# A decoder layer on one core: rotation moved, raw weight loads moved, two retention products on split operands, three evictions on VectorE

## The chip, the cores and the metric

The kernel runs on one core of a Trainium2 chip. The metric is the device time of one execution in microseconds (us). The engines are TensorE (PE: matrix products and transposes), VectorE (DVE), ScalarE (ACT), GpSimd (POOL) and SyncE (SP). Each has its own queue and works through it in order. SP issues most of the loads; POOL issues most of the stores and some loads.

## The reference

One layer of a hybrid decoder is computed for a prompt of 1024 positions and for 8 samples of 4 positions each, with 1024 channels, all in float32:

```python
h = rms_norm(x, g_pre_mix) @ w_in      # q, k, v of attention; q, k, v, gate of retention; two merge gates
o_a = sliding-window attention (128), 8 heads on 2 key/value heads, with sinks
qr, kr = rope_ret(q_r), rope_ret(k_r)  # x * cos + rot * sin, rot swaps neighbouring channels
# retention, 4 heads, chunks of 128 positions, state s of 128 x 256 per head:
scores = (q @ k.T) * dmask
o   = scores @ v + (q @ s) * q_decay
s   = gamma**128 * s + (k * k_decay).T @ v
o_r = silu(gate) * head_rms(o)
mixed = (sigmoid(gm_a) * (o_a @ w_a_proj) + sigmoid(gm_r) * (o_r @ w_r_proj)) @ w_o
x = x + rms_norm(mixed); x = x + rms_norm(conv_ffn(rms_norm(x)))
```

The outputs are the layer's results for both groups, and the new caches and states.

## The kernel before, in words

**Split products.** Most products are made of split operands. `split` (L227) writes a rounded copy `hi` of a float32 tile with ACT, in the type fp32r, and the remainder `lo = x - hi` with DVE (the operation is in `ew`, L220, whose DVE form is line L223 of the profile). `mm3` (L254) then makes three fp32r matmuls out of them: hi times hi, hi times lo, lo times hi (L255, L256, L257). A few products, those of the retention blocks among them, are made in one float32 matmul without a split.

**The stream.** After attention, the rest of the input projection (retention's q and k, its gate, the two merge gates) is made by a generator, `stream` (L901 on). It works through 16 pairs of column blocks in the order `ORDER`. For each pair and each half `j` of the positions it makes seven products in the order A11, S1, A22, S2, A12, S4, S3 (a seven-product scheme for 2 x 2 blocks); the product A22 of a half is made inside the next half. A product is 12 matmuls of 264 columns. `adv(n)` advances the stream by n products, and the other stages call it between their own steps, so that their short products stand among the stream's. `nxt[p] = next(ws)` prepares the operand of the next pair as soon as the product that used the same buffer has been made; the eviction of the accumulators in the banks `q0`, `q1`, `q2` is ACT's (L927, L948) and DVE's (L950, L952).

**Raw weights.** `in_split` (L812) loads the two raw tiles of a pair (L819) on SP's queue, each with a `yield` after it, and then makes the seven weight operands by sums and splits (`w_split`, L331 and L223). The generator of the pair after next is called `coming`. Up to the end of the sample group's blocks the raw tiles take turns in two buffers, from then on in three. The first raw tile is last read by the sum `a21 = a11 - a21`, which is part of the S3 step; the second by the split of `a22`.

**Rotation.** A half of a retention q/k pair is finished in `post_qk` (L853): SP loads the neighbouring channels into two `sh` tiles (L860) when `flush()` is called, at the S2 product of the next half. The second step, `turned`, is put on the list `LATER`: six DVE operations (times cosine, times sine, sum, for q and for k) and a store to `qk_d` on POOL's queue (L868). It is called at the S1 product of the half after.

**The sample group's retention** (`sample`, L1040) runs among products of the stream, first head after `adv(4)` and `adv(20)`. It loads states from DRAM, splits them into `s0s`, and adds products with them (L1078, L1083).

**The prompt's retention** has 32 blocks (4 heads of 8 chunks). `front` makes the scores and transposes k in one bank (L1164, L1165), DVE multiplies by the mask into `sT` (L1167), ACT by the decay into `kt` (L1169). `middle` makes three float32 products of 256 columns: scores with v (L1177), q with the state (L1179), k with v (L1181); DVE updates the state (L1184, L1186), and `finish` normalizes with ACT and POOL (L1017 to L1022). `tail` transposes back (L1028) and multiplies by the gate (L1200). In the loop, block g+1 has its `front` before block g has its `middle`, with four products of the stream per block. `load_qk` (L1138) and `load_v` (L1145) are issued three blocks ahead, into five buffers each.

**The attention projection** (`attn_proj`, L779) makes eight half tiles `y_a` in three chunks each; ACT evicts each chunk (L786) out of two PSUM buffers.

**Order.** A planner goes over the whole program, takes what is ready by its own model of the durations, earlier program text first, and so fixes the order on every engine's queue; it also places the waits. What is written next to each other need not stay so.

Of the kernel before, what the change touches and what calls it, by code (L numbers as in the profile page):

```python
# [10 lines left out]
F32R = mybir.dt.float32r  # L11
# [7 lines left out]
P = 128  # L19
# [101 lines left out]
def trunk(ctx, tc, I, O):  # L121
# [657 lines left out]
    def attn_proj(mm):  # L779
        def src(r0):  # L780
            return w_a[r0:r0 + 256, 256 * mm:256 * mm + 256].rearrange("(g d) n -> d g n", d=64)
        w = weights(4, 256, [(lambda r: r[0:64], src(0)), (lambda r: r[64:128], src(256))])
        for half in range(2):
            y = p2.tile([P, T], F32, name="y_a", bufs=2)
            for c0, n in CHUNKS[1:] + CHUNKS[:1]:
                S.copy(out=y[:, c0:c0 + n], in_=gemm_chunk(w, actA, c0, n, 4, half * P, ps_a()))  # L786
            st.dma_start(out=gm_d[2 * mm + half], in_=y)
# [113 lines left out]
    def stream():  # L901
# [8 lines left out]
        for i, n in enumerate(ORDER):  # L910
            for j in range(2):
# [17 lines left out]
                for p in (A11, S1, A22, S2, A12, S4, S3):  # L929
                    if p == A22:  # L930
                        if last is not None:
                            product(A22, *last)
                        if j == 0 and i:
                            ops[A22] = next(ws)
                            ws = coming
                            if i + 1 < len(ORDER):
                                next(ws)
# [15 lines left out]
                    if p == S2:  # L953
                        flush()
                    if p == S1 and LATER:
                        LATER.pop()()
# [6 lines left out]
                    if j and i + 1 < len(ORDER):  # L963
                        nxt[p] = next(ws)
                        if p == S4 and i + 2 < len(ORDER):
# [131 lines left out]
    adv(20)  # L1097
# [35 lines left out]
    def load_qk(g):  # L1133
# [3 lines left out]
        qks[g] = ST("qk", (P, 2, P), bufs=5)  # L1137
        ld.dma_start(out=qks[g], in_=qk_d[h].rearrange("i p t -> p i t")[:, :, cols(tt)])  # L1138

    def load_v(g):  # L1140
# [3 lines left out]
        vts[g] = ST("vt", (P, 256), bufs=5)  # L1144
# [14 lines left out]
    def front(g, dm):  # L1159
# [6 lines left out]
        sT = ST("sT", (P, P), bufs=2)  # L1166
        V.tensor_tensor(out=sT, in0=ps[:, :P], in1=dm, op=mult)  # L1167
        kt = ST("kt", (P, P), bufs=2)
        S.mul(kt, ps[:, P:2 * P], kdec[:, 0, h:h + 1])  # L1169
        return ps, sT, kt, vt, q  # L1170

    def middle(g, ps, sT, kt, vt, q):
# [4 lines left out]
        TE.matmul(po, sT, vt, start=True, stop=tt == 0)  # L1177
# [3 lines left out]
        TE.matmul(pk, kt, vt, start=True, stop=True)  # L1181
# [53 lines left out]
    def ahead(g):  # L1235
# [4 lines left out]
        load_qk(g + 3)  # L1240
        load_v(g + 3)
        return front(g, state["dm"])

    for g in range(3):
        load_qk(g)
    for g in range(3):
        load_v(g)
    adv(0)
    coming, behind = ahead(0), None
    for g in range(NBLK):  # L1250
        f, coming = coming, ahead(g + 1)
# [3 lines left out]
        m = middle(g, *f)  # L1255
        adv(1)
# [6 lines left out]
    adv(len(ORDER) * 14 - 8 - 82 - 4 * NBLK - 1)  # L1263
# [526 lines left out]
```

## Time and profile before

| | us |
|---|---|
| median of 3 runs | 1656.74 (1656.53 to 1758.46) |
| profiled execution | 1658.69 |
| its span, first to last instruction | 1656.9 |
| PE busy | 1626.7 (98%) |
| DVE busy | 1205.9 (73%) |
| ACT busy | 863.6 (52%) |
| POOL busy | 446.3 (27%) |

The page and the answers of the trace come from the one profiled execution; a line such as L223 is a line of the kernel. "Busy" of PE overlaps, since matmuls are pipelined: the distance of their starts tells what one costs. Waits name the engine and line that waited, behind the arrow what released it. The stages that the change touches lie at these places of the span: the attention projection from about 237 us, the stream and the sample group's retention from about 300 to 450 us, the prompt's retention from about 450 to 686 us.

### The profile page before, as it was taken

The page shows a single profiled execution, that of the slowest core. Times are in us where ns is not written, and L with a number is a line of the kernel's source. Part 1 is how long each engine was busy: PE and PEld are TensorE (multiplying, and loading weights), DVE is VectorE, ACT ScalarE, POOL GpSimd, SP SyncE. Part 2 cuts the span into 40 slices and gives each one's busy share as a digit, 9 for nine tenths or more (in the row PEclk, how much of TensorE's full clock was granted, in tenths as well). Part 3 has the DMA queues.
Part 4 walks back from the last instruction along what each step waited for, and adds up shares of the span by engine and source line. Part 5 has one row for each costly group of instructions (what it writes and reads, how often), then busy time and mean ns, then how long its engine had stood idle before and what let it go on. Part 6 is the DMA issues. An engine that isn't in the chain of part 4 may idle for free.

```text
span 1656.9 us, 32509 instructions
## 1 busy us (share of the span) xinstructions
PE 1626.7 (98%) x12551; PEld 1589.6 (96%) x12551; DVE 1205.9 (73%) x2035; ACT 863.6 (52%) x1882; POOL 446.3 (27%) x654
## 2 busy tenths in 40 slices
PE   8999999999999999999999999999999999999997
PEld 7999999999999999999789999999999999999997
DVE  7878749688565655569748988988988988445476
ACT  6565634456565655564424655555555556443343
POOL 4232431012233332243312422321231322111111
PEclk9999999999999999999999999999999999999999
DMA  7212235556677665697422245454545548766664
GB/s 201 65 49 71 72 80 193 185 187 191 207 230 235 197 216 156 209 309 234 157 89 89 59 148 173 161 162 160 182 136 177 173 150 253 237 196 198 194 186 145
DMA packets 275852, 278.22 MB, mean 168 GB/s; under 512 B 23552, under 2 KB 234784, under 8 KB 275681
## 3 DMA queue, kind: packets, MB, share of 16 engines
q1 hardware_dynamic: 241937, 159.58, 33.2%
q0 software_dynamic: 33760, 116.57, 20.1%
q8 instruction: 98, 1.61, 0.4%
q14 instruction: 57, 0.47, 0.1%
HBM read 184.24 MB, written 87.49 MB: 164 GB/s over the span
## 4 chain that ended last, share of the span: by engine, by line
PE 71%; DMA 3%; DVE 1%; issue 1%; ACT 0%; POOL 0%; DVEq 0%; POOLq 0%; SPq 0%
PE ps_m L255 10%; PE ps_m L257 10%; PE ps_m L256 10%; PE ps_t L256 8%; PE ps_t L255 8%; PE ps_t L257 8%; PE ps_q L255 4%; PE ps_q L257 4%; PE ps_q L256 4%; PE ps_b L1177 1%; PE ps_a L1181 1%; PE ps_b L1179 1%; DMA w_raw<-in_w_in 1%; DMA t<-in_w_o 1%; DMA vt<-v_d 0%
## 5 line engine op out<-in xcount | busy, mean ns | idle before, releaser
L255 PE MATMUL ps_t<-xh,w_hi 128*128 128x264 f32 (+2 forms) x524 | 148.9, 284 | 0.0
L223 DVE SCALAR_TENSOR_TENSOR w_lo<-w_raw,w_hi 128x1024 fp32r<-128x1024 f32 x82 | 103.6, 1268 | 62.0 <-ACT w_hi L228 57.2
L256 PE MATMUL ps_t<-xl,w_hi 128*128 128x264 f32 (+2 forms) x524 | 148.7, 284 | 0.0
L257 PE MATMUL ps_t<-xh,w_lo 128*128 128x264 f32 (+2 forms) x524 | 148.0, 283 | 0.0
L257 PE MATMUL ps_m<-xh,w_lo 128*128 128x264 f32 x512 | 145.4, 284 | 0.6 <-DVE w_lo L223 0.6
L255 PE MATMUL ps_m<-xh,w_hi 128*128 128x264 f32 x512 | 145.8, 285 | 0.0
L256 PE MATMUL ps_m<-xl,w_hi 128*128 128x264 f32 x512 | 145.4, 284 | 0.0
L223 DVE SCALAR_TENSOR_TENSOR w<-w_raw,w 128x512 fp32r<-128x512 f32 x152 | 104.2, 685 | 38.4 <-ACT w L331 38.0
L1537 DVE SCALAR_TENSOR_TENSOR c_out<-u_ext,fconst,c_out 128x1024 f32<-128x1024 f32 x96 | 121.9, 1280 | 2.1 <-ACT c_out L1533 0.3
L255 PE MATMUL ps_q<-xh,w 128*128 128x264 f32 x384 | 114.2, 297 | 3.1 <-DVE pair L950 3.1
L255 PE MATMUL ps_q<-ex,w 128*128 128x264 f32 x384 | 114.0, 297 | 0.6 <-DVE pair L952 0.6
L228 ACT CAST w_hi<-w_raw 128x1024 fp32r<-128x1024 f32 x62 | 65.2, 1052 | 92.7 <-PE ps_t L256 80.0
L256 PE MATMUL ps_q<-ex,w 128*128 128x264 f32 x384 | 110.6, 288 | 0.0
L256 PE MATMUL ps_q<-xl,w 128*128 128x264 f32 x384 | 110.5, 288 | 0.0
L257 PE MATMUL ps_q<-xh,w 128*128 128x264 f32 x384 | 110.4, 288 | 0.0
L257 PE MATMUL ps_q<-ex,w 128*128 128x264 f32 x384 | 109.8, 287 | 0.0
L331 ACT CAST w<-w_raw 128x512 fp32r<-128x512 f32 x152 | 94.7, 623 | 15.7 <-PE ps_q L257 8.2
L257 PEld LDWEIGHTS ps_t<-xh,w_lo 128*128 128x128 f32 x524 | 98.7, 188 | 0.0
L256 PEld LDWEIGHTS ps_t<-xl,w_hi 128*128 128x128 f32 x524 | 98.6, 188 | 0.0
L255 PEld LDWEIGHTS ps_t<-xh,w_hi 128*128 128x128 f32 x524 | 98.6, 188 | 0.0
L257 PEld LDWEIGHTS ps_m<-xh,w_lo 128*128 128x128 f32 x512 | 96.3, 188 | 0.8 <-DVE w_lo L223 0.8
L255 PEld LDWEIGHTS ps_m<-xh,w_hi 128*128 128x128 f32 x512 | 96.2, 188 | 0.0
(450 smaller groups left out, 6072.6 us busy)
## 6 DMA issues: line engine op xcount, KB each, us to landing
w_raw<-in_w_up SPq DMA_DIRECT2D x48, 512.0 KB, 4.3
w_raw<-in_w_in SPq DMA_DIRECT2D x42, 512.0 KB, 4.2
w_raw<-s_d SPq DMA_DIRECT2D x60, 256.0 KB, 4.1
t_d<-t POOLq DMA_DIRECT2D x24, 528.0 KB, 4.0
t<-t_d POOLq DMA_DIRECT2D x24, 528.0 KB, 4.9
t<-in_w_down SPq DMA_DIRECT2D x48, 256.0 KB, 5.2
s_d<-t POOLq DMA_DIRECT2D x24, 512.0 KB, 3.6
w_raw<-in_w_down SPq DMA_DIRECT2D x36, 256.0 KB, 5.1
```

The lines of the kernel that those rows point to most:

```text
L223: pinned(V.scalar_tensor_tensor(out=out, in0=in0, scalar=1.0, in1=in1, op0=mult, op1=op))
L228: pinned(S.copy(out=hi, in_=src))
L255: TE.matmul(ps, wh, xh, start=start, stop=False, **kw)
L256: TE.matmul(ps, wh, xl, start=False, stop=False, **kw)
L257: TE.matmul(ps, wl, xh, start=False, stop=stop, **kw)
L331: S.copy(out=t[:, 0:4], in_=src)
L1177: TE.matmul(po, sT, vt, start=True, stop=tt == 0)
L1179: TE.matmul(po, q, state["s"], start=False, stop=True)
L1181: TE.matmul(pk, kt, vt, start=True, stop=True)
L1537: V.scalar_tensor_tensor(out=c[:, NS:], in0=u[:, g, NU + t:NU + t + SEQ], scalar=sc[t], in1=c[:, NS:], op0=mult, op1=add)
```

## The change

- `attn_proj`: the three chunks of the first half tile are evicted by DVE; the other 21 by ACT as before.
- `stream`: the second step of the rotation is called at the S2 product, ahead of `flush()`, and no longer at S1.
- `stream`: the second raw tile of the pair after next is loaded right after the S3 operand is prepared (the first one is loaded one product earlier, at S4, as before), and no longer at the next half's A22.
- The sample group starts after 22 products instead of 20; what is left after the prompt's blocks is two products fewer.
- Retention blocks: `sT` and `kt` become the two halves of one tile `sk`. A new function `parts` splits `v` and `sk`; it is called for the next block after the `middle` of the present one. Its four results have one buffer each. The products L1177 and L1181 become `mm3`, three fp32r matmuls each; the product with the state stays in float32.
- `load_qk` and `load_v` run two blocks ahead instead of three, with four and three buffers instead of five each.

```diff
@@ attn_proj
-                S.copy(out=y[:, c0:c0 + n], in_=gemm_chunk(w, actA, c0, n, 4, half * P, ps_a()))
+                ps = gemm_chunk(w, actA, c0, n, 4, half * P, ps_a())
+                if mm or half:
+                    S.copy(out=y[:, c0:c0 + n], in_=ps)
+                else:
+                    V.tensor_copy(out=y[:, c0:c0 + n], in_=ps)
@@ stream
                             ops[A22] = next(ws)
                             ws = coming
-                            if i + 1 < len(ORDER):
-                                next(ws)
...
                     if p == S2:
+                        if LATER:
+                            LATER.pop()()
                         flush()
-                    if p == S1 and LATER:
-                        LATER.pop()()
...
                         nxt[p] = next(ws)
+                        if p == S3 and i + 2 < len(ORDER):
+                            next(coming)
                         if p == S4 and i + 2 < len(ORDER):
                             coming = in_split(ORDER[i + 2])
                             next(coming)
@@
-    adv(20)
+    adv(22)
@@ load_qk, load_v
-        qks[g] = ST("qk", (P, 2, P), bufs=5)
+        qks[g] = ST("qk", (P, 2, P), bufs=4)
...
-        vts[g] = ST("vt", (P, 256), bufs=5)
+        vts[g] = ST("vt", (P, 256), bufs=3)
@@ front
-        sT = ST("sT", (P, P), bufs=2)
-        V.tensor_tensor(out=sT, in0=ps[:, :P], in1=dm, op=mult)
-        kt = ST("kt", (P, P), bufs=2)
-        S.mul(kt, ps[:, P:2 * P], kdec[:, 0, h:h + 1])
-        return ps, sT, kt, vt, q
-
-    def middle(g, ps, sT, kt, vt, q):
+        sk = ST("sk", (P, 2 * P), bufs=2)
+        V.tensor_tensor(out=sk[:, :P], in0=ps[:, :P], in1=dm, op=mult)
+        S.mul(sk[:, P:], ps[:, P:2 * P], kdec[:, 0, h:h + 1])
+        return ps, sk, vt, q
+
+    def parts(ps, sk, vt, q):
+        s, v = ([ST(n + b, (P, 256), F32R) for b in "hl"] for n in ("s", "v"))
+        split(*v, vt)
+        split(*s, sk)
+        return ps, s, v, q
+
+    def middle(g, ps, sk, vt, q):
...
-        TE.matmul(po, sT, vt, start=True, stop=tt == 0)
+        mm3(po, *(x[:, :P] for x in sk), *vt, True, tt == 0)
...
-        TE.matmul(pk, kt, vt, start=True, stop=True)
+        mm3(pk, *(x[:, P:] for x in sk), *vt, True, True)
@@ the loop over blocks
-        load_qk(g + 3)
-        load_v(g + 3)
+        load_qk(g + 2)
+        load_v(g + 2)
...
-    for g in range(3):
+    for g in range(2):
         load_qk(g)
-    for g in range(3):
+    for g in range(2):
         load_v(g)
     adv(0)
-    coming, behind = ahead(0), None
+    f, behind = parts(*ahead(0)), None
     for g in range(NBLK):
-        f, coming = coming, ahead(g + 1)
+        coming = ahead(g + 1)
...
         m = middle(g, *f)
+        f = parts(*coming) if coming else None
...
-    adv(len(ORDER) * 14 - 8 - 82 - 4 * NBLK - 1)
+    adv(len(ORDER) * 14 - 8 - 84 - 4 * NBLK - 1)
```

## The prediction

> **What bounds the kernel now.** I read the page first, then the waits of TensorE's own queue, then the stretches of time by stage, then the order of events around each of those waits.
>
> ```profile
> PE 1626.7 (98%) x12551; PEld 1589.6 (96%) x12551; DVE 1205.9 (73%) x2035; ACT 863.6 (52%) x1882; POOL 446.3 (27%) x654
> PE 71%; DMA 3%; DVE 1%; issue 1%; ACT 0%; POOL 0%; DVEq 0%; POOLq 0%; SPq 0%
> ```
>
> TensorE (PE) is busy 98% of the span, and the chain that ended last is PE nearly throughout. So the change can pay in two ways only: less PE work, or fewer of the few PE waits.
>
> ```profile
> PE ps_q L255 <- DVE pair L950: 3.1, 2, 2.1
> PE ps_b L1078 <- DVE s0s L223: 2.1, 1, 2.1
> PE ps_b L1028 <- ACT o L1022: 1.5, 1, 1.5
> PE ps_a L255 <- ACT y_a L786: 1.5, 1, 1.5
> PE ps_q L255 <- DVE pair L952: 0.6, 1, 0.6
> ```
>
> Columns: who waited for whom, us in total, times, longest. These five are the longest waits of PE in the stages that the change touches, 8.8 us together. The stages themselves:
>
> ```profile
> 330.00:360.00 30.00, 26.93 (x209) 26.48 (x208) 25.32 (x47) 14.84 (x39) 4.51 (x7) 0.94 0.55 185
> 395.00:430.00 35.00, 31.99 (x250) 31.70 (x251) 21.68 (x40) 23.06 (x59) 6.00 (x9) 0.96 0.64 200
> 475.00:570.00 95.00, 95.00 (x728) 92.86 (x728) 53.13 (x118) 57.10 (x142) 39.09 (x67) 1.00 0.66 207
> 570.00:685.00 115.00, 115.00 (x886) 112.69 (x885) 65.75 (x140) 63.85 (x159) 35.88 (x60) 1.00 0.54 173
> ```
>
> Columns: length, then PE, PEld, DVE, ACT and POOL busy, the granted clock, DMA share. The last two rows are the prompt's retention blocks: PE never idle, VectorE (DVE) at 56 and 57%, ScalarE (ACT) at 60 and 56%. The first two, inside the sample group's stage, have PE idle for 3 us each, and a clock below 1: 30 us x 0.06 = 1.8 us and 35 us x 0.04 = 1.4 us are lost to it. The one wait of 2.1 us in each stretch stands ahead of it:
>
> ```profile
> 351.02 0.56 PE L1078 MATMUL ps_b<-s0s,q 128*64 128x256 f32 x3 [2.09 <-DVE s0s L223]
> 351.59 0.28 PE L256 MATMUL ps_q<-xl,w 128*128 128x264 f32 x1
> 351.71 0.31 PE L257 MATMUL ps_q<-xh,w 128*128 128x264 f32 x1
> 352.04 0.42 PE L256 MATMUL ps_q<-xl,w 128*128 128x264 f32 x1
> 352.26 0.42 PE L257 MATMUL ps_q<-xh,w 128*128 128x264 f32 x1
> ```
>
> Matmuls that start 0.12 us apart are 0.22 us apart soon after the wait. I price such a wait at 2.1 + 1.6 = 3.7 us (1.6 is the mean of 1.8 and 1.4). The Trainium skill, "TensorE: Matmul & The Clock Gate", Part 1 on the clock gate, says the clock halves after an idle window of about 3.4 us; by it a 2.1 us wait would cost 2.1 us alone. The granted clock of these stretches speaks against that.
>
> **Split operands in two block products.** Each of 32 blocks has three fp32 products, of which the first (L1177) and third (L1181) become three fp32r matmuls each; the second, with the state, stays.
>
> ```profile
> 527.00 0.59 PE L1177 MATMUL ps_b<-vt,sT 128*128 128x256 f32 x2
> 527.43 0.59 PE L1179 MATMUL ps_b<-state,qk 128*128 128x256 f32 x2
> 527.86 0.59 PE L1181 MATMUL ps_a<-vt,kt 128*128 128x256 f32 x2
> 534.68 0.59 PE L1177 MATMUL ps_b<-vt,sT 128*128 128x256 f32 x2
> 431.89 0.28 PE L1083 MATMUL ps_a<-v,kb 128*128 128x256 f32 x1
> 432.01 0.28 PE L256 MATMUL ps_q<-ex,w 128*128 128x264 f32 x1
> ```
>
> Durations overlap in the pipeline; starts count. One fp32 product takes 0.43 us (527.00 to 527.43). An fp32r matmul of the same 256 columns, L1083, gives way after 0.12 us. Three are 0.36 us, so 0.07 us is saved per product, 0.14 us per block, 4.5 us in 32 blocks. With 0.118 to 0.125 us as what rounding leaves of 0.12, the bounds are 3.5 and 4.9 us. As PE is the bound there, this goes straight into the span.
>
> The price is two ACT casts and two DVE subtractions of 128x256 per block (the merged operand `sk` replaces two writes by two). Nearest rows:
>
> ```profile
> 682.09 0.47 ACT L1022 ACTIVATE o<-ps_b,rs 128x256 f32<-128x256 f32 x1 [0.24 <-POOL rs L1021]
> 685.84 0.42 ACT L228 CAST xh<-z 128x264 fp32r<-128x264 f32 x1
> 686.94 0.43 DVE L223 SCALAR_TENSOR_TENSOR xl<-z,xh 128x264 fp32r<-128x264 f32 x1
> 679.47 0.59 PE L1177 MATMUL ps_b<-vt,sT 128*128 128x256 f32 x2
> ```
>
> That is 64 x 0.43 = 27.5 us of DVE and 64 x 0.42 = 27 us of ACT in some 245 us (32 blocks of 7.68 us, 527.00 to 534.68), which takes both to about 68 to 70%. Nothing waits in the loop: the splits stand behind the block's normalization, which ends 3.1 us after the block's first product (682.56 against 679.47); two casts and the last subtraction make it 4.4 us; the next block's products come at 7.6 us. The single buffers of the split halves are free by then too, because the state update ahead of them on DVE already waits for the same third product. Cover 3.2 us; if it is gone, PE waits for what is missing, once a block.
>
> Shorter leads: a `vt` is now wanted about 2.5 blocks (19 us) and a `qk` 2 blocks (15 us) after its issue; issue to landing took
>
> ```profile
> DMA to landing us min/median/max: 2.3/3.8/8.3
> DMA to landing us min/median/max: 2.2/4.0/11.5
> ```
>
> (`vt`, then `qk`). Both fit; zero.
>
> **Entry of the retention.** The first `vt` has no such lead. It used to be read by PE alone, in the block's first product. Now ACT's in-order queue reads it right behind `front`, with all of ACT's evictions behind it and, on DVE, bank evictions L950 and L952. A DVE that stood waiting for a landing shows both ends:
>
> ```profile
> 449.94 0.69 DVE L223 SCALAR_TENSOR_TENSOR s<-w_raw 128x512 f32<-128x512 f32 x1 [3.12 <-DMA w_raw<-in_w_in]
> 425.54 0.69 DVE L223 SCALAR_TENSOR_TENSOR s<-w_raw 128x512 f32<-128x512 f32 x1 [5.25 <-DMA w_raw<-in_w_in]
> ```
>
> The 3.12 us cost PE nothing, the 5.25 us became the 2.1 us wait for L950 and its clock, 3.7 us. The longest `vt` landing was 8.3 us. I take +1.0 us, nearer the lower row, since ACT may have other work ahead of it; bounds 0 and +3.7. I exclude a gain: nothing is removed there but two early loads.
>
> **Rotation's second step later.**
>
> ```profile
> 349.03 0.71 DVE L223 SCALAR_TENSOR_TENSOR pair<-pair,rcos 128x528 f32<-128x528 f32 x1 [4.56 <-DMA sh<-pair]
> 350.28 0.68 DVE L223 SCALAR_TENSOR_TENSOR s0s<-s,s0s 128x512 fp32r<-128x512 f32 x1
> 345.86 0.62 ACT L228 CAST s0s<-s 128x512 fp32r<-128x512 f32 x1
> 343.79 1.18 SPq L860 DMA_DIRECT2D sh<-pair  x2
> ```
>
> DVE stood 4.56 us waiting for the neighbour rows, with the sample's state split queued behind it, whose other half ACT had ready at 346.5; that split is what PE waited for at 351.02. The step now comes two products (2 x 1.46 us: 12 starts of 0.12) later. But it also frees the two `sh` buffers later, so the loads of the next half, which SP issues as they come free, move with it: of 2.9 us hardly one is left as lead. The sample blocks move by the same two products (22 for 20), so the order of this step against them need not change either. Best case: this wait with its clock and one of the L950 waits (3.1 - 2.1 = 1.0 us) go, -4.7 us. Worst: nothing. I take -2.0, a little under half. Its store on GpSimd's queue moves alike with the normalizations' steps there, so zero. Two products fewer stand between the last block and the end of the stream; PE's one wait there is the 0.6 us for L952, so zero, at most the two products, 2.9 us.
>
> **Raw weights earlier.** In the retention the second load comes three products earlier; DVE's waits for it there cost no PE time (clock and PE are full). In the stage before, only two raw buffers exist, and the load at 418 us, the cause of the 5.25 us wait, was issued as its buffer came free:
>
> ```profile
> 418.30 0.37 SPq L819 DMA_DIRECT2D w_raw<-in_w_in  x1
> 417.58 0.69 DVE L223 SCALAR_TENSOR_TENSOR w<-w_raw,w 128x512 fp32r<-128x512 f32 x1 [1.58 <-ACT w L331]
> ```
>
> (417.58 + 0.69 = 418.27.) It can't come sooner. Zero, at best -3.7 us by chance of order.
>
> **First projection tile on VectorE.** PE waited 1.5 us for ACT's eviction at
>
> ```profile
> 250.24 0.86 ACT L786 COPY y_a<-ps_a 128x384 f32<-128x384 f32 x2
> 249.89 0.55 DVE L223 SCALAR_TENSOR_TENSOR qS<-o,qS 128x32 fp32r<-128x32 f32 x4 [6.71 <-ACT qS L228]
> ```
>
> DVE is idle 6.71 us before, so it can evict earlier; but the product that waits also needs the sample columns split at 249.89 to 250.44. I take -0.3 us; bounds -1.5 and +0.5 (evictions queued behind the split). The three evictions, about 0.43 us each as on ACT, delay the operand sums behind them on DVE by 1.3 us; the projection's other 21 chunks hide that.
>
> **Sum:** -4.5 + 1.0 - 2.0 - 0.3 = -5.8 us. The profiled execution took 1658.69 us, its span 1656.9 us and 1.8 us around it; it lies 1.95 us over the median of 1656.74. So 1652.9 us there, and 1651 us as a median.
>
> **Rivals.**
>
> First, the stalls go as a whole: -4.9 - 4.7 - 1.5 - 3.7 = -14.8, 1642 us. For it: each hangs on the order of a few instructions. Against it: the raw load's buffer and the sh buffers above.
>
> Second, the moved steps change nothing, because the planner already interleaves the six operations of the rotation with others (the split follows two of them at 350.28), and the entry costs its whole 3.7 us: -4.5 + 3.7, 1656 us. The later steps then don't do what they say.
>
> Third, slower: in the sample's stage the second raw load now stands ahead of the split that frees its buffer, by three products, 4.4 us, on SP's in-order queue. State loads and `qk` loads queue behind; if they land late, a split of `s0s` is late as at 350.28, 3.7 us each time. The sample's 56 products span four steps of 14, so up to four times: +14.8 - 5.8 = +9, 1666 us; from two times on it decides. Against it:
>
> ```profile
> SPq L819 <- DVE w7x L223: 57.3, 6, 19.4
> SPq L1038 <- DMA out_ret_sample<-s: 28.6, 9, 9.1
> ```
>
> SP waits up to 19.4 us on raw buffers already, without a PE wait that names a state load.
>
> **Numbers.** Chances: forecast (1646 to 1655) 0.50, first rival 0.15, second 0.22, slower 0.13. The range 1642 to 1660 us takes in the bounds: below, the first rival; above, -3.5 with the entry's +3.7 and 2.9 us at the end of the stream, +3.1. Over 2% is 33 us, about what a measurement of this kernel can tell from no change; no case reaches it, and I leave 0.02 faster and 0.03 slower for order upset elsewhere.
>
> **What will show it.** L1177 and L1181 with three starts of 0.12 us each, a block of 7.54 us; DVE near 69% there with no PE wait for L223 on the split halves. PE waits at the entry for L950 or L927 behind a `vt` landing: my +1.0. The wait for `s0s` and the lower clock near 350 us: gone or still there decides the rotation. A block pitch of 7.7 us or more, or SP holding state loads, would prove me wrong.

## The result, and the profile after

The changed kernel takes 1666.04 us (median), the kernel before 1656.74 us in the runs made beside it: a ratio of 1.0055, 95% interval 1.0041 to 1.0068. It is slower by 9 us, where a gain of 6 us was forecast; that is within 2%, as forecast, but 6 us above the upper end of the range. Executions that stand far above the others of their kernel, as the 1758.46 us in the table of before, are left out of all ratios. The profiled execution of the changed kernel took 1666.49 us, its span is 1664.7 us. In the changed kernel's lines L950 and L952 (bank evictions by DVE) have become L952 and L954, L927 is L931, L786 is L788 with DVE's form at L790, and the merge's L1287 to L1304 are L1297 to L1314.

The page of the changed kernel, busy time and the chain of waits:

```profile
PE 1626.6 (98%) x12615; PEld 1590.9 (96%) x12615; DVE 1229.7 (74%) x2102; ACT 875.4 (53%) x1943; POOL 454.1 (27%) x654
PE 85%; DVE 6%; DMA 5%; issue 2%; ACT 2%; SPq 1%; POOL 0%; DVEq 0%; ACTq 0%; POOLq 0%
```

PE is still the bound, with the same busy time. The shares of DVE and DMA in the chain have grown (from 1 and 3%), but so has that of PE (from 71%), so the chain alone does not tell where the time went. PE's waits in the changed kernel (total, times, longest):

```profile
PE ps_q L255 <- DVE pair L952: 5.9, 4, 2.3
PE ps_m L255 <- DVE Gr L1312: 2.7, 1, 2.7
PE ps_q L255 <- DVE pair L954: 2.5, 2, 1.9
PE ps_a L255 <- DVE y_a L790: 1.9, 1, 1.9
PE ps_t L255 <- DVE Gr L1314: 1.3, 2, 0.9
PE ps_m L255 <- DVE Gr L1314: 1.2, 1, 1.2
```

Beside the list of before, the wait for `s0s` is gone, the bank evictions cost 8.4 us instead of 3.7, and the three `Gr` rows are new: they lie in the merge, a stage that the change does not touch. The next fence has the stretches of the changed kernel (length; PE, PEld, DVE, ACT, POOL busy; granted clock; DMA share; GB/s):

```profile
252.00:256.00 4.00, 4.00 (x17) 4.00 (x16) 3.28 (x5) 0.00 (x0) 0.57 (x1) 0.57 0.69 207
400.00:406.00 6.00, 4.55 (x24) 4.55 (x25) 4.44 (x9) 4.34 (x10) 0.97 (x2) 0.72 0.51 158
475.00:570.00 95.00, 95.00 (x772) 94.21 (x771) 61.75 (x145) 65.20 (x170) 37.02 (x64) 1.00 0.65 205
570.00:685.00 115.00, 115.00 (x937) 114.26 (x937) 78.38 (x177) 72.15 (x196) 40.47 (x65) 1.00 0.55 179
```

The blocks (last two rows) run as before with PE full. The first two rows are new places with a slow clock.

To see where time went, I cut the span at PE's own marks: first and last product of the attention projection, first and last product of the sample group, first and last `front`, first product on z, first output product. The planner also lets stream matmuls change stages, so a longer stage need not be a loss. Each difference below is therefore the stage's length minus that of before, less 0.122 us (1.46 us / 12) for each stream matmul that the stage has more than before. All in us, from the one profiled execution of each kernel:

```
                               projec-  to samples  sample  blocks  last front  merge   rest
                               tion     begin       group           to z
length before                  61.1     32.0        115.7   212.7   36.5        82.7    868.7
changed kernel                 +2.0     +1.7        -4.3    -1.7    +3.4        +7.6    -0.4
```

(The 10.9 us between sample group and first front are left out: the changed kernel has ten matmuls more in it and no wait.) Up to the end of the blocks the change gains 2.3 us by these two executions; the -4.3 of the sample group is no firm gain, since that stage scatters by some 4 us between executions (shown below). After the blocks, where the prediction had put zero, it loses 11 us.

Most of the loss after the blocks has one visible root. SyncE (SP) issues the loads of the next stage: two raw tiles of the projection weights, z, then three pairs of merge operands `g_in` and `a_in`, then raw tiles three and four. The order of events on SP, in the kernel before (start and length in us, line, operation, what it loads, how often):

```profile
690.77 0.69 SPq L1287 DMA_DIRECT2D g_in<-gm_d  x1
698.61 5.84 SPq L316 DMA_DIRECT2D w_raw<-in_w_r_proj  x4
```

In the changed kernel raw tile three stands ahead of the merge operands, and SP, which takes its queue in order, is held at it for a free buffer (8.0 us, until DVE's split of an earlier tile ends; SP, and last a row of ACT):

```profile
689.86 9.62 SPq L316 DMA_DIRECT2D w_raw<-in_w_r_proj  x3
699.53 0.57 SPq L1297 DMA_DIRECT2D g_in<-gm_d  x1
705.13 1.49 SPq L316 DMA_DIRECT2D w_raw<-in_w_r_proj  x2
718.81 1.05 ACT L228 CAST w_hi<-w_raw 128x1024 fp32r<-128x1024 f32 x1 [5.45 <-DMA w_raw<-in_w_r_proj]
```

The first `g_in` is issued 8.8 us later than before, raw tile four behind it, and ACT stands 5.45 us for that tile, which it casts at 718.81 (before, the cast of the fourth tile stood at 712.97). What that does to the merge stage is seen some 60 us later. The first and the fifth 15 us of the stage, before and after:

```profile
705.00:720.00 15.00, 15.00 (x125) 15.00 (x125) 8.15 (x7) 11.67 (x18) 3.36 (x5) 1.00 0.99 326
765.00:780.00 15.00, 14.44 (x118) 14.23 (x117) 15.00 (x23) 5.96 (x12) 6.48 (x4) 1.00 0.72 221
```

```profile
706.00:721.00 15.00, 15.00 (x125) 15.00 (x125) 4.86 (x4) 7.76 (x12) 2.24 (x3) 1.00 1.04 351
766.00:781.00 15.00, 11.18 (x85) 10.32 (x84) 14.20 (x16) 8.26 (x16) 10.95 (x6) 1.00 0.81 263
```

PE is full in the first row of both. But DVE has done 4.9 us of work instead of 8.2 and ACT 7.8 instead of 11.7: splits that are due sooner or later. The DMA engines are busy throughout there in both kernels (share 0.99 and 1.04), which leaves little room to make it up by loading faster. At the end of the stage, when DVE is the full engine anyway (15.00 of 15 before), PE drops from 14.4 to 11.2 us busy. My reading is that the missing work then stands in front of DVE's evictions; the two executions alone do not show it.

### The profile page after: what moved, and what is told of

Its sections match the earlier page's. It is cut to its first block, busy times and chain, and to the rows that moved or that the text cites. A ratio compares the mean times of both kernels' runs of the same rounds, so it can differ in the third digit from the quotient of the medians.

```text
span 1664.7 us, 32842 instructions
## 1 busy us (share of the span) xinstructions
PE 1626.6 (98%) x12615; PEld 1590.9 (96%) x12615; DVE 1229.7 (74%) x2102; ACT 875.4 (53%) x1943; POOL 454.1 (27%) x654
## 4 chain that ended last, share of the span: by engine, by line
PE 85%; DVE 6%; DMA 5%; issue 2%; ACT 2%; SPq 1%; POOL 0%; DVEq 0%; ACTq 0%; POOLq 0%
PE ps_m L257 9%; PE ps_m L255 9%; PE ps_m L256 9%; PE ps_t L256 8%; PE ps_t L255 8%; PE ps_t L257 8%; PE ps_q L255 5%; PE ps_q L257 5%; PE ps_q L256 5%; PE ps_mm L255 2%; PE ps_mm L256 2%; PE ps_mm L257 2%; PE ps_a L255 1%; PE ps_a L256 1%; PE ps_a L257 1%
## 5 line engine op out<-in xcount | busy, mean ns | idle before, releaser
L255 PE MATMUL ps_q<-xh,w 128*128 128x264 f32 x384 | 111.5, 290 | 5.9 <-DVE pair L952 5.9
L257 PE MATMUL ps_q<-xh,w 128*128 128x264 f32 x384 | 109.6, 285 | 0.0
```

The costliest lines, as they stand in the source:

```text
L255: TE.matmul(ps, wh, xh, start=start, stop=False, **kw)
L257: TE.matmul(ps, wl, xh, start=False, stop=stop, **kw)
```

## The experiments

Each number below is a median with its ratio to the kernel before, run beside it; 0.001 is 1.7 us. The lengths of stages are reckoned as in the table above, from one profiled execution of each kernel. That execution can lie 4 us from the kernel's median (1672.03 against 1667.92 us with the eviction undone, 1652.88 against 1656.92 with the shift in the other direction), so a stage's number shows a place, and the medians decide.

**First: is it the exit, or the split products?** The theory was that the two products taken from the exit upset the order of the next stage's loads; the rival, that the split operands load ACT and DVE too much.

The shift undone, the rest of the change kept:

```diff
-    adv(22)
+    adv(20)
...
-    adv(len(ORDER) * 14 - 8 - 84 - 4 * NBLK - 1)
+    adv(len(ORDER) * 14 - 8 - 82 - 4 * NBLK - 1)
```

> The changed kernel with the two-product shift undone: the sample group starts after 20 products again, and two products more are left after the prompt's blocks; the other parts of the change stay. Exit theory (the loss of 7.6 us between the last block and the output projection comes from the prompt's blocks ending two products nearer to the end of the stream, so that the next stage's raw weights, operands and gate inputs are loaded in another order and later): about 1658 us, 8 us less than the changed kernel, with the merge stage as before. Split theory (the longer ACT and DVE queues of the split operands delay the exit): about 1666 us. Rotation: the sample's first head could now wait for its q and k, up to +3 us.

Measured: 1658.97 us, 1.0020 (1.0008 to 1.0031). The merge stage is at +0.4 us and the stretch before it at +0.7. What is left over the kernel before stands ahead of the samples (projection +1.9, then +1.9).

The split products and shorter leads alone, on the kernel before (the diff's `parts`, `mm3`, `sk`, `load_qk` and `load_v` hunks):

```diff
+    def parts(ps, sk, vt, q):
...
-        load_qk(g + 3)
+        load_qk(g + 2)
```

> The kernel before with the split operands and the shorter leads alone. Exit theory: the blocks give their 4 to 4.5 us, the entry takes 1 to 3 us, the merge stage is untouched: 1653 to 1656 us. Split theory: the merge stage loses its 7 us here too: 1660 us or more.

Measured: 1652.17 us, 0.9980 (0.9968 to 0.9991): faster than both kernels. The blocks are 2.7 us shorter.

The moved steps without the split (rotation, raw weights, shift, eviction on DVE), shown against the changed kernel:

```diff
-        mm3(po, *(x[:, :P] for x in sk), *vt, True, tt == 0)
+        TE.matmul(po, sT, vt, start=True, stop=tt == 0)
```

> The change without the split operands and shorter leads: rotation later, two-product shift, raw load earlier, evictions on VectorE. Exit theory: the merge stage loses 7 us here too and the blocks gain nothing: 1664 to 1670 us. Split theory: 1654 to 1659 us.

Measured: 1667.99 us, 1.0074 (1.0058 to 1.0090), merge +6.4. The split theory fell with these three: the split gains, and what loses is among the moved steps.

The front half of the shift kept, the exit as before (the two products are saved at the end of the sample group instead):

```diff
-    adv(2)
     turns.pop()()
...
-    adv(len(ORDER) * 14 - 8 - 84 - 4 * NBLK - 1)
+    adv(len(ORDER) * 14 - 8 - 82 - 4 * NBLK - 1)
```

> The whole change, sample group after 22 products, but the two products that stood between the sample group and the prompt's blocks taken out and put back behind the blocks, so that only the distance of the blocks from the end of the stream is as before. Exit theory: the merge stage as before, about 1658 us. Split theory: 1666 us. Both: the entry may cost 0 to 3 us more, since the blocks begin right behind the sample group.

Measured: 1660.98 us, 1.0026 (1.0016 to 1.0036). The stretch before the merge is back (-0.3), the merge itself only partly (+4.2), although from 676 us to the end of the merge every queue, the last block's own products apart, has the order of the kernel before again. Raw tile three is issued 6.8 us ahead of the first product on z in both kernels. Its cast on ACT starts 0.5 us behind that product in the kernel before, and 5.0 us behind it here, after a wait for the transfer (ACT, before and here):

```profile
705.91 1.05 ACT L228 CAST w_hi<-w_raw 128x1024 fp32r<-128x1024 f32 x1
709.34 1.05 ACT L228 CAST w_hi<-w_raw 128x1024 fp32r<-128x1024 f32 x1 [4.40 <-DMA w_raw<-in_w_r_proj]
```

So with one order of work the merge took 82.7 us in one profiled execution and 86.9 in another, and the late landing of one transfer is the first difference of more than 1 us between them. Why it landed late is open.

**Second: the parts one by one.**

The first projection tile back on ACT:

```diff
-                if mm or half:
-                    S.copy(out=y[:, c0:c0 + n], in_=ps)
-                else:
-                    V.tensor_copy(out=y[:, c0:c0 + n], in_=ps)
+                S.copy(out=y[:, c0:c0 + n], in_=ps)
```

> The changed kernel with the attention projection's first tile back on ScalarE. Queue theory: the three evictions of that tile stand on VectorE behind the splits of qS and the 1.25 us sums; TensorE's wait there grew from 1.46 to 1.86 us and the clock then halved for 3.4 us, so this part alone costs the 2.5 us by which the projection stage of the changed kernel is longer. Undone, the stage is as long as before (61.1 us between its first and last product instead of 63.6), the half clock at 252 us is gone, and the time is 1663 to 1664 us beside a kernel before at 1656. Rival, the later waits take the gain back, since the first product of the samples waits for its own data: 1666 us, and the stage from the last projection product to the first sample product grows by 2.5 us.

Measured: 1667.92 us, 1.0062 (1.0041 to 1.0084). The projection stage is as long as before, as expected, but nothing is gained: the sample group is 6.5 us worse than in the changed kernel (+2.2 against -4.3) and PE waits 3.0 us at the first `front` for its `qk` load. The rival had the sum about right and its place wrong.

The rotation's second step back at S1:

```diff
-                    if p == S2:
-                        if LATER:
-                            LATER.pop()()
-                        flush()
+                    if p == S2:
+                        flush()
+                    if p == S1 and LATER:
+                        LATER.pop()()
```

> The changed kernel with the rotation's second step back at its old place (after S1). Queue theory: in the changed kernel the rotation at 325.9 us waits 3.7 us for its sh transfer with the bank evictions queued behind it, and TensorE waits 2.3 us; back at its old place that wait has no eviction behind it, and the stage from the last projection product to the first sample product is within 1 us of the 32.0 us of before instead of 35.4. In the sample stage the wait for s0s near 350 us with the half clock after it (3.7 us in all) comes back. Both together: 1664 to 1667 us, no gain by undoing it. Rival, the raw loads' new place makes the 3.4 us: the stage stays at 35.4 us, and the time at 1666 us or above.

Measured: 1666.94 us, 1.0058 (1.0036 to 1.0079). The sum was as expected, the places were not: the stretch to the first sample product became longer still (+4.6), and the wait for `s0s` did not come back. PE waits 3.5 us for a bank eviction at 328.5 us there, so that wait is not made by the rotation's step.

The raw weights back at A22:

```diff
                             ws = coming
+                            if i + 1 < len(ORDER):
+                                next(ws)
...
-                        if p == S3 and i + 2 < len(ORDER):
-                            next(coming)
```

> The changed kernel with the raw weight loads back in their old place behind A22. Queue theory: the stage to the first sample product stays at about 35.4 us, the exit stays late, since it needs only the two products' shift (merge stage 90.4 us instead of 82.8), and the time is 1664 to 1667 us. Rival, the raw loads at their new place hold SyncE's queue (the third rival of the prediction): the stage to the first sample product is 32 us again, the entry's 1.2 us is gone too, and the time is 1661 to 1662 us.

Measured: 1669.39 us, 1.0074 (1.0052 to 1.0096). Neither the samples nor the merge (+9.0) gets better: the raw loads' new place is not what costs.

The eviction alone, on the kernel before:

```diff
+                if mm or half:
+                    S.copy(out=y[:, c0:c0 + n], in_=ps)
+                else:
+                    V.tensor_copy(out=y[:, c0:c0 + n], in_=ps)
```

> The kernel before with one part of the change: the attention projection's first tile evicted by VectorE. Queue theory: the projection stage is 2.5 us longer with a half clock at 252 us, and the time is 1658 to 1659 us beside 1656. Rival, its cost is taken back by the next stage's waits, or it is nothing without the other parts: 1655.5 to 1656.5 us.

Measured: 1660.84 us, 1.0024 (1.0011 to 1.0037). The projection is 1.9 us longer, and 1.7 us follow before the samples begin. So alone it costs some 4 us, more than either expectation, and inside the change undoing it brings nothing.

**Third: the shift by itself, and the order at the exit.** To set the order back, z's loads were first put three products earlier:

```diff
-    adv(len(ORDER) * 14 - 8 - 84 - 4 * NBLK - 1)
+    adv(len(ORDER) * 14 - 8 - 84 - 4 * NBLK - 1 - 3)
```

> The changed kernel with the loads of z issued three products earlier in the program's text, straight behind the last tail; every queue is the same as in the changed kernel up to the end of the 32 blocks, and on SyncE the three pairs of merge loads (g_in, a_in) now stand ahead of the third raw tile of the projection weights, as in the kernel before. Exit theory: the merge stage (first product on z to first output product) takes 83 to 84 us instead of 90.4, and the time is 1659 to 1660 us beside 1656.5. Rival, the order on SyncE doesn't matter, since the DMA engines are full there whatever comes first: the stage stays above 88 us and the time is 1664 us or more.

Measured: 1671.97 us, 1.0098 (1.0085 to 1.0111). The split of z writes into the operand tiles `X`, which the stream's last three products still read; here they read z in place of the input, so this kernel no longer computes the layer, and they wait for it (one wait of 5.9 us for `xh`). So the stretch before the merge pays 10.8 us for a dependence of its own, and the total is no test. The merge stage alone, with the three merge pairs ahead of raw tile three, is at +1.4.

The shift alone, on the kernel before:

```diff
-    adv(20)
+    adv(22)
...
-    adv(len(ORDER) * 14 - 8 - 82 - 4 * NBLK - 1)
+    adv(len(ORDER) * 14 - 8 - 84 - 4 * NBLK - 1)
```

> The kernel before with the two products moved from the exit to the front of the sample stage (22 and 84), nothing else. Exit theory: SyncE gets the third raw tile ahead of the merge loads, the merge stage takes 89 to 91 us instead of 82.8, and the time is 1661 to 1664 us beside 1656.5. Rival, the shift is harmless without the other parts: 1656 to 1657 us and a merge stage of 83 us.

Measured: 1670.97 us, 1.0088 (1.0073 to 1.0103). The shift alone costs 15 us, more than the whole change does and far more than was expected. The profiled execution shows 10 of them: the merge has 5.5, the sample group 2.1, the first `front` 2.7.

The shorter leads alone (`load_qk`, `load_v` and their buffers):

```diff
-        load_v(g + 3)
+        load_v(g + 2)
```

> The kernel before with the shorter leads alone (qk and v two blocks ahead instead of three, four and three buffers). If the split products made the gain of the split-only kernel, this one is at 1656 to 1657 us, with the blocks' stage as long as before (212.8 us from the first to the last front). Rival one, the shorter leads gave that gain: 1652 to 1653 us. Rival two, the entry of the blocks pays for them, as the prediction bounded it: up to 3.7 us between the last sample product and the first front, and 1658 to 1660 us.

Measured: 1655.40 us, 0.9993 (0.9982 to 1.0003). They cost nothing. A gain of their own of up to 3 us is not excluded by the interval, but the blocks are only 0.7 us shorter here, against 2.7 with the split, so most of the gain is the split's.

Split, leads and rotation:

```diff
                     if p == S2:
+                        if LATER:
+                            LATER.pop()()
                         flush()
-                    if p == S1 and LATER:
-                        LATER.pop()()
```

> The kernel before with the split products, the shorter leads and the rotation's second step at S2; no shift, no move of the raw weights, no eviction on VectorE. If the rotation's move is worth what the prediction's first rival gave it (the wait for s0s near 347 us and the half clock after it, 3.7 us in all): 1648 to 1650 us, beside 1652 for the split alone. Rival, the move puts the wait for the sh transfer ahead of bank evictions and TensorE waits there instead, as at 325 us in the changed kernel: 1652 to 1656 us.

Measured: 1652.87 us, 0.9985 (0.9975 to 0.9995), the split's gain and no more.

The clean test of the order at the exit: in the changed kernel the three merge pairs are requested in the text ahead of raw tile three, and both are pinned in that order. PE's whole order is unchanged.

```diff
+            if pi == 0 and c == 0:
+                for m, half in [(2 * c_ + e_ + 4 * MERGE[p_][0], MERGE[p_][1]) for p_ in PORD if p_ in MERGE
+                                for c_ in range(2) for e_ in range(2)][:3]:
+                    early[m, half] = ga_load(m, half, True)
...
+            if w is w_r and pt == 0 and (p, c) == (A12, 0):
+                pin(ins)
```

> The changed kernel with only the order of loads at the exit set back: the three pairs of merge loads (g_in, a_in) are pinned ahead of the third raw tile of the projection weights on SyncE; TensorE's whole order is that of the changed kernel. Exit theory: the merge stage takes 83 to 84 us instead of 90.4, nothing before it changes, and the time is 1659 to 1660 us beside 1656. Rival, the order does not matter because what is late is the mass of transfers at the exit: the stage stays above 88 us, the time at 1665 us or more.

Measured: 1659.56 us, 1.0018 (1.0010 to 1.0027), and a merge stage of +0.1. SP's queue and the two stretches of the merge in this kernel:

```profile
691.20 2.79 SPq L1301 DMA_DIRECT2D g_in<-gm_d  x1
699.68 6.63 SPq L316 DMA_DIRECT2D w_raw<-in_w_r_proj  x4
```

```profile
707.00:722.00 15.00, 15.00 (x126) 15.00 (x125) 7.77 (x7) 11.86 (x19) 3.16 (x5) 1.00 0.99 312
767.00:782.00 15.00, 14.44 (x116) 14.12 (x116) 15.00 (x23) 5.94 (x12) 6.50 (x4) 1.00 0.69 221
```

The first `g_in` is issued at 691 us again, DVE and ACT do their 7.8 and 11.9 us in the first stretch, and PE has its 14.44 us in the fifth. This kernel has only these loads exchanged in its text and keeps the whole order of PE; the planner then also places some work of DVE, ACT and GpSimd in the merge differently. With that, some 6 us of the 9 are gone, and the two intervals lie apart: that the order at the exit makes them is shown. The stretch before the merge is still at +3.4, so that part is not theirs.

How a late load becomes a wait of PE is read off the traces, not tested. In all twenty profiled executions of this document it goes with DVE's work in the first 60 us after the first product on z: where DVE has done 42.9 to 46.2 us of work by then, the merge takes 82.5 to 83.1 us (ten kernels, the one before among them); where it has done 39.0 to 42.1, the merge takes 84.1 to 91.7 (ten kernels, the changed one with 39.8). The first 15 us alone do not tell: the kernel with split and rotation has 7.1 us of DVE work there and a merge of 82.8 us, the one with the shift in the other direction 7.9 and 87.1.

The two halves of the shift, each on the kernel before. Front: 22 products ahead of the samples, the two taken from the end of the sample group:

```diff
-    adv(20)
+    adv(22)
...
-    adv(2)
     turns.pop()()
```

> The kernel before with 22 products instead of 20 ahead of the sample group, and the two taken from the end of the sample stage; the exit is as before. If the front half of the shift makes the stalls of the shift-only kernel (2.3 us in the sample stage, 3.9 us between the last sample product and the first front, where the first block waits for its qk load): 1660 to 1662 us, with both. If the whole price of the shift is at the exit: 1655 to 1657 us.

Exit: the two products from the exit to the end of the sample group:

```diff
-    adv(2)
+    adv(4)
     turns.pop()()
...
-    adv(len(ORDER) * 14 - 8 - 82 - 4 * NBLK - 1)
+    adv(len(ORDER) * 14 - 8 - 84 - 4 * NBLK - 1)
```

> The kernel before with two products moved from the exit to the end of the sample stage, after the last sample step; the start of the sample group is as before. Exit theory: the merge stage is 5 to 8 us longer (88 to 91 us instead of 82.8), the stages before it as before, and the time is 1661 to 1664 us. If the exit is harmless without the front half: 1655 to 1657 us.

Measured: front 1664.75 us, 1.0054 (1.0040 to 1.0069); exit 1664.41 us, 1.0053 (1.0034 to 1.0071). Each costs 9 us, the front more than expected. The exit kernel has it in the merge (+7.6) and before it (+1.4). The front kernel has +2.5 in the samples, +2.1 in the blocks and 2.6 at the first `front`, where PE waits for a load that SP issued 8 us later than before. The order of events on PE and SP of the front-only kernel, then on SP of the kernel before:

```profile
463.62 0.77 PE L1163 MATMUL ps_a<-qk 128*128 128x128 f32 x2 [2.42 <-DMA qk<-qk_d]
454.42 4.80 SPq L1137 DMA_DIRECT2D qk<-qk_d  x5
```

```profile
446.16 3.55 SPq L1138 DMA_DIRECT2D qk<-qk_d  x5
```

The changed kernel does not show this wait. The eviction on DVE goes with its absence: of the ten profiled kernels with 22 products ahead of the samples, the seven with that eviction have no wait there, and the three without it wait 2.4 to 3.0 us. I have not followed by what.

Split and leads, with the shift in the other direction:

```diff
-    adv(20)
+    adv(18)
...
-    adv(len(ORDER) * 14 - 8 - 82 - 4 * NBLK - 1)
+    adv(len(ORDER) * 14 - 8 - 80 - 4 * NBLK - 1)
```

> Split products and shorter leads as in the split-only kernel (1652), and the shift in the other direction: 18 products ahead of the sample group and two more at the exit (80). If the shift hurts because of the order it brings (merge loads behind the third raw tile, sample stage and first qk load late), the other direction keeps the merge stage at 83 us and costs nothing: 1649 to 1653 us. If any other place of the sample group is worse than the one of before, whose order was fitted to it: 1656 us or more.

Measured: 1656.92 us, 1.0006 (0.9995 to 1.0017), the second of the two: it loses the split's gain. So a shift in either direction costs. The profiled execution has a merge of +4.4 although SP has the three merge pairs ahead of raw tile three; I have not traced that.

Split and leads with the raw weights' new place, and the whole change without shift and eviction:

```diff
+                        if p == S3 and i + 2 < len(ORDER):
+                            next(coming)
```

> Split products, shorter leads and the raw weights' new place; no shift, no rotation move, no eviction on VectorE. If the raw weights' move is free, as the prediction had it: 1651 to 1654 us beside 1656, the same as the split alone (1652). If it holds other loads on SyncE (the third rival of the prediction): 1656 us or more. If it is worth the 3 us by which undoing it made the changed kernel longer: 1648 to 1650 us.

> The whole change without the shift and without the eviction on VectorE: split products, shorter leads, rotation at S2, raw weights behind the freeing split. If the shift and the eviction are what costs: 1650 to 1654 us beside 1656, faster than both kernels. Rival, the rotation at S2 makes TensorE wait for bank evictions before the first sample product also without the shift: that stage is 3 us longer, and the time 1655 us or more.

Measured: 1653.20 us, 0.9986 (0.9975 to 0.9998), and 1653.18 us, 0.9990 (0.9978 to 1.0002). The moves of rotation and raw weights are worth nothing on top of the split; the loss is not theirs.

## Why the prediction was wrong, step by step

**What bounds the kernel**: right. PE stayed at 98%, and the time gained or lost is PE work, PE waits and the half clock behind some of them. (PE's 71% of the chain was less than the "nearly throughout" that I read there.)

**Split operands, -4.5 us**: right. Block products of the changed kernel:

```profile
530.27 0.28 PE L255 MATMUL ps_b<-vh,sh 128*128 128x256 f32 x1
530.38 0.28 PE L256 MATMUL ps_b<-vl,sh 128*128 128x256 f32 x1
537.79 0.28 PE L255 MATMUL ps_b<-vh,sh 128*128 128x256 f32 x1
```

The starts are 0.11 to 0.12 us apart, and the block's pitch is 7.52 us (7.54 forecast). DVE stands at 67% in the two block rows above, with no wait for a split half in the steady loop. In the split-only kernel the blocks gain 2.7 us; with PE's waits in them taken off (2.3 us against 0.7 before) they are 4.3 us shorter, and the stretch behind them, with the last block's products, 0.3.

**Entry, +1.0 us (0 to 3.7)**: right in mechanism, a little low. ACT and PE of the split-only kernel:

```profile
452.93 0.41 ACT L228 CAST vh<-vt 128x256 fp32r<-128x256 f32 x1 [3.65 <-DMA vt<-v_d]
456.33 0.39 PE L255 MATMUL ps_q<-ex,w 128*128 128x264 f32 x1 [1.46 <-ACT pair L927]
```

ACT stands 3.65 us for the first `vt`, its evictions come behind, and PE waits 1.46 us for one of them, without a clock loss. In the changed kernel PE's waits in the first two blocks are 0.80, 1.21 and 0.52 us, 2.5 together.

**Rotation later, -2.0 us**: failed as a cause. "The wait for `s0s` and the lower clock near 350 us: gone or still there decides the rotation", I wrote. It is gone, but not by this step. It is gone too with the step undone, and with the step moved on top of the split alone it is there (1.0 us, and 2.0 with the raw weights moved as well). The eight profiled kernels that have neither 22 products ahead of the samples nor the eviction on DVE all have it (1.0 to 2.3 us); in the twelve that have either, it is gone or down to 0.5. In its place PE waits for bank evictions. DVE and PE of the changed kernel:

```profile
325.92 0.71 DVE L223 SCALAR_TENSOR_TENSOR pair<-pair,rcos 128x528 f32<-128x528 f32 x1 [3.73 <-DMA sh<-pair]
327.16 0.42 DVE L952 TENSOR_TENSOR pair<-ps_q,pair 128x264 f32<-128x264 f32 x1
327.64 0.39 PE L255 MATMUL ps_q<-xh,w 128*128 128x264 f32 x1 [2.13 <-DVE pair L952]
401.45 0.39 PE L255 MATMUL ps_q<-xh,w 128*128 128x264 f32 x1 [2.29 <-DVE pair L952]
```

The rotation still waits 3.7 us for its transfer, now with the bank evictions next behind it, and PE waits for them, once more at 401.45. The wait at 327.64 comes with the first projection tile on DVE: all nine profiled kernels with that eviction wait 1.9 to 3.5 us for a bank eviction there, the kernel with the eviction alone (2.2) and the one with the rotation's step undone (3.5) among them, and none of the eleven others does. The step's own worth, alone on the split, is nothing (0.9985 against 0.9980).

**Raw weights, 0**: right (0.9986 against 0.9980). So the third rival fell as a mechanism, though its time, 1666 us, is the one that was measured. It came from another place.

**First projection tile, -0.3 us (-1.5 to +0.5)**: failed. I named "evictions queued behind the split" as the bad end and put 0.5 us on it. They are queued so, behind the split and then the third behind two sums, 1.25 us each:

```profile
249.48 0.55 DVE L223 SCALAR_TENSOR_TENSOR qS<-o,qS 128x32 fp32r<-128x32 f32 x4 [6.72 <-ACT qS L228]
250.06 1.02 DVE L790 COPY y_a<-ps_a 128x384 f32<-128x384 f32 x2
253.33 0.45 DVE L790 COPY y_a<-ps_a 128x288 f32<-128x288 f32 x1
250.76 0.37 PE L255 MATMUL ps_a<-qS,w_hi 128*128 128x288 f32 x1 [1.86 <-DVE y_a L790]
```

The wait itself grew by 0.4 us only, from 1.46 to 1.86 us. What I left out is the clock: in the row 252.00:256.00 above it is 0.57, 0.43 x 4 = 1.7 us lost. Together that is the 2.0 us of the table. And the wait at 327.64 above comes with this step too, at a place where I did not look. Alone it costs some 4 us.

**Two products fewer at the exit, "zero, at most the two products, 2.9 us"**: this is the step that failed most. I looked at PE's waits in that stretch and found 0.6 us to lose. I did not ask what the two products are for the planner: two products' time in which SP's next loads come free in another order. The stretch before the merge lost 3.4 us (a wait of 1.94 us for L954 at 694.81, and its clock) and the merge 7.6; with the order of the loads set back, the merge's 7.6 are gone. The term had to include the queues of the stage that follows.

**The front half of the shift** I took to move the sample group "by the same two products", as a whole and at no price. Alone it costs 9 us; 2.6 of them are PE's wait for the late `qk` load, and the rest I have not traced. In the change the other parts hide most of that: with the exit as before, 22 products cost 2 us more than 20 (1660.98 against 1658.97).

One thing bears on all these readings: in the sample group single executions of one order differ by some 4 us. Its length is 115.7 us in the profile of before, 112.1 with the split alone and 111.4 with the leads alone, and in these three every queue is the same up to the loads of the first blocks. The profile that I read for the prediction is the longest of them. A term of -2.0 us that is read off one wait in that stage is within this scatter.

## What to carry to other kernels

Where a planner orders the queues, moving work between stages is no sum of removed and added waits: look at the in-order DMA queue at the seam, and ask which load now stands ahead of which and for what buffer it will hold the queue. A stage can run full for 60 us on a debt: the engine that is behind (here DVE, 3.3 us less done in the first 15 us and 5.0 less after 60) shows it before PE waits. And price parts that save work apart from parts that move it: here the split alone gained 3 us, and everything that moved took 12 away.

## What the runs showed of the hardware

**A short wait can cost its length again in clock, but not always.** In the changed kernel the 1.86 us wait in the projection is followed by matmuls 0.32 us apart (384 columns) where they had been 0.17 apart. The same wait, of the same 1.86 us, in the kernel with the merge loads set back, on PE:

```profile
251.10 0.37 PE L255 MATMUL ps_a<-qS,w_hi 128*128 128x288 f32 x1 [1.86 <-DVE y_a L792]
252.09 0.29 PE L256 MATMUL ps_a<-qS,w_hi 128*128 128x288 f32 x1
252.22 0.30 PE L257 MATMUL ps_a<-qS,w_lo 128*128 128x288 f32 x1
```

There the matmuls keep their 0.13 us, and the projection is 0.5 us longer instead of 2.0. This 1.86 us wait stands in nine of the profiled kernels; in eight the clock halves behind it, in this one it does not. Nor did it behind the 2.13 us wait at 327.64 in the changed kernel (granted clock 1.00 from 323 to 336 us). The Trainium skill, "TensorE: Matmul & The Clock Gate", Part 1, says that the clock is decided in free-running windows of some 3.4 us and falls after an idle one. That it depends on where a wait falls fits these runs, and the loss fits the window: 1.7 us is what half clock costs in 3.4 us. That a whole window must be idle does not fit, for waits of 1.86, 1.94 and 2.29 us were enough.

**DVE and GpSimd hold each other up in the merge.** DVE and POOL of the changed kernel:

```profile
773.42 1.54 DVE L223 SCALAR_TENSOR_TENSOR xl<-Gr,xh 128x264 fp32r<-128x264 f32 x1
783.26 0.42 DVE L223 SCALAR_TENSOR_TENSOR xl<-Gr,xh 128x264 fp32r<-128x264 f32 x1
772.45 2.23 POOL L1300 TENSOR_TENSOR Gr<-Gr,g_in 128x528 f32<-128x528 f32 x1 [0.71 <-DVE Gr L1314]
762.90 1.32 POOL L1300 TENSOR_TENSOR Gr<-Gr,g_in 128x528 f32<-128x528 f32 x1 [16.66 <-DVE Gr L1314]
```

The same subtraction takes 1.54 us while a GpSimd merge runs and 0.42 us when none does, and the merge 2.23 us against 1.32. The Trainium skill, "SBUF — State Buffer", states that a VectorE instruction with two inputs there and a GpSimd instruction that reads there exclude each other for the whole instruction, and the rows agree. The kernel before has such rows too (subtractions of 1.57 and 1.56 us, GpSimd merges of up to 2.32), so they are no loss that the change brought.
